# An expert layer's gathered tokens: 72 instead of 64, with GpSimd issuing the small transfers

## The chip, the cores and the metric

The program runs on one core of one Trainium2 chip. The metric is the device time of one execution in microseconds (us), taken as the median over runs. TensorE (PE in the profile) multiplies, VectorE (DVE) and ScalarE (ACT) do the elementwise work, GpSimd (POOL) issues the indirect transfers, and SyncE (SP) issues all the large loads. The engines have one program each, and each runs its own in order.

## The reference, cut to what matters

A two-layer transformer block, a mixer block with cross attention, and a layer of product-key experts run over 256 tokens of width 1024. The change lies in the last of these. Each token picks 16 experts for each of 8 heads, 128 experts in all out of 16384, each with a gate. An expert is a row of `peer_u` and a row of `peer_v`:

```python
act = jax.nn.gelu(jnp.einsum('thkd,td->thk', peer_u[eb], xb), approximate=False) * gb
return jnp.einsum('thk,thkd->td', act, peer_v[eb])
```

So token t gets the sum over its 128 experts of gelu(u·x) · gate · v.

## The kernel before

Everything ahead of `phase_peer` is untouched. In `phase_peer` the 256 tokens go two ways.

**The dense way, 192 tokens (TD).** All 16384 experts are computed for them. A loop of 128 columns j loads one 128x1024 tile of u (512 KB, by SP) for 128 experts and multiplies it with the tokens' x, which is the moving operand. 82 of the columns are plain: 8 chunks of one float32 product of 192 columns (L1648), each of which the trace shows as two passes. The other 46 are split into a high and a low part by ACT (L216) and DVE (L217), which gives 8 pairs of a product of 384 columns (L1650) and one of 192 (L1651). The results stand in A, [128 experts, 128 columns, 192 tokens]. The gates reach A through products of one-hot tables, four tokens at a time (L1531 to L1564, with L1557 on PE); this begins at column J0 = 75, since the end of A holds the routing's tables until then. A second loop of 128 columns does the same with v, always split, in 8 pairs of 384 and 192 columns (L1701, L1702), into eight PSUM banks. At its end a column's sums are halved together, transposed back, added to x, normed and written.

**The gathered way, 64 tokens (TS), the last ones.** Their 128 experts each lie in 64 columns of a table `es` over 128 partitions: partitions 64 to 127 hold a token's second 64 experts, partitions 0 to 63 hold the first 64. The gates lie likewise in `gs`, and `x2` holds the tokens' x twice. A row step gathers 128 rows of u by an indirect transfer from GpSimd (L1474, 512 KB); three steps later DVE multiplies them with `x2` and sums (L1459) into one column of `hs`. After 64 steps come gelu and gates, then 64 steps with rows of v, which DVE adds up weighted (L1464) into `sacc`. At the end the halves are joined: a transfer from SP brings the sums on partitions 0 to 63 to the others (L1486), and DVE adds both to x (L1488, L1490). The rows have four buffers.

**What sets the order.** Every engine's order is fixed when the program is built. `Pace` spreads the row steps over the columns: 33 over columns 12 to 74, 53 over columns 75 to 127, 48 over the first 112 columns of the v loop. A gather also waits for the last product of the column in which it is written (`beat`). The picks of the gathered tokens (`routing(1)`) are made during the projection that precedes the loops and the first 12 columns; `gather(1)` then fills `es` and `gs` by three small transfers from SP (L1424 to L1426), which wait for DVE in SP's queue, ahead of the loads of u that stand behind them. `x2` is filled by one such transfer (L1505).

Of the kernel before, what the change touches and what calls it, by code (L numbers as in the profile page):

```python
# [19 lines left out]
T = 256  # L20
# [81 lines left out]
def layout(I):  # L102
# [91 lines left out]
class K:  # L194
# [12 lines left out]

    def granule(self, ap, w=1024, raw=None):
# [4 lines left out]
        hi = self.ring.tile([128, 1024], F32R, name="hi", bufs=3)  # L213
        lo = self.ring.tile([128, 1024], F32R, name="lo", bufs=3)
# [1092 lines left out]
def phase_peer(k, pool, wpool, out):  # L1307
# [5 lines left out]
    TS = 64  # L1313
    TD = T - TS
    S0 = 128 - TS
# [24 lines left out]

    es = wpool.tile([128, 64], I32, name="es", bufs=1)
    gs = wpool.tile([128, 64], F32, name="gs", bufs=1)
    hs = wpool.tile([128, 64], F32, name="hs", bufs=1)
    x2 = wpool.tile([128, D], F32, name="x2", bufs=1)

# [60 lines left out]
    def gather(tt):  # L1406
# [11 lines left out]
        if tt == 1:  # L1418

            own = slice(S0, 128)  # L1420
            e = slot(8, 64).bitcast(I32)
            V.scalar_tensor_tensor(e[own], ri[own, 0:64], 128.0, rj[own, 0:64], op0=OP.mult, op1=OP.add)
            V.scalar_tensor_tensor(es[own], ri[own, 64:128], 128.0, rj[own, 64:128], op0=OP.mult, op1=OP.add)
            nc.sync.dma_start(es[0:S0], e[own])  # L1424
            nc.sync.dma_start(gs[0:S0], bv[own, 0:64])
            nc.sync.dma_start(gs[own], bv[own, 64:128])  # L1426
        ps = k.tp()
# [17 lines left out]
    def behind(i, how):  # L1445
        k.tc.add_manual_dep(i.ins, beat[0].ins.name, mybir.DependencyInfo(how, mybir.DependencyReason.DATA), reason="pace")


    def gathered():
        AHEAD = 3  # L1450
        todo = []
        sacc = None

        def take():
            nonlocal sacc
# [11 lines left out]
            if (kind, c) == ("u", 63):  # L1467
# [17 lines left out]
        low = wpool.tile([128, D], F32, name="row", bufs=4)  # L1485
        nc.sync.dma_start(low[S0:128], sacc[0:S0])  # L1486
        x = k.x[S0:128, 1, :]
        V.tensor_tensor(x, x, sacc[S0:128], OP.add)  # L1488
        yield
        V.tensor_tensor(x, x, low[S0:128], OP.add)  # L1490
        yield

    J0 = 75
    early, late = routing(1), routing(0)
    for c in range(16):
# [3 lines left out]
        if c == 12:  # L1499
# [3 lines left out]
            V.tensor_scalar(xn[1], k.x[:, 1, :], inv[:, 1:2], None, op0=OP.mult)  # L1503
            V.tensor_tensor(x2[S0:128], xn[1][S0:128], gpeer[S0:128], OP.mult)
            nc.sync.dma_start(x2[0:S0], x2[S0:128])  # L1505

# [100 lines left out]
    for c in range(8):  # L1607
        ps = k.tp()
        nc.tensor.transpose(ps[:, 0:128], xn[0][:, c * 128:c * 128 + 128], k.ident)
        nc.tensor.transpose(ps[:, 128:TD], xn[1][0:S0, c * 128:c * 128 + 128], k.ident[0:S0, 0:S0])  # L1610
        col = k.gains[:, GCOL["peer"] + c:GCOL["peer"] + c + 1]
# [105 lines left out]
    last = [column(j) for j in range(128 - LAST, 128)]  # L1717
    oT = A[:, 6:14, :]
    part = A[:, 40:48, :]
# [4 lines left out]
    def turn(c):  # L1724
# [88 lines left out]
```

## Time and profile before

| | us |
|---|---|
| three runs, median | 1751.54 |
| lowest and highest | 1749.48, 1752.36 |
| the profiled execution, its own time | 1753.15 |
| its span, first to last instruction | 1751.4 |
| PE busy | 1711.7 (98%) |
| DVE busy | 1311.6 (75%) |
| ACT busy | 997.6 (57%) |
| POOL busy | 249.5 (14%) |

The time of the profiled execution is 1.75 us longer than its span, and 1.6 us over the median. PE's busy time is a poor guide, because products are pipelined and their ends are modelled. What counts is the step from one product's start to the next, and the places where PE sat idle. The two loops take the last 697 us of the span.

### The profile page before, as it was taken

What the parts mean: (1) busy time and instruction counts of PE and PEld (TensorE: products, weight loads), DVE (VectorE), ACT (ScalarE), POOL (GpSimd) and SP (SyncE); (2) the same over time, 40 slices, a digit from 0 to 9 for tenths busy, and PEclk for the clock granted to TensorE, in tenths of its full rate; (3) what the DMA queues carried; (4) which work ended last, traced back from release to release, by engine and by line L of the source; (5) the groups of instructions that cost most, each with busy time, mean ns of one, the idle gap of its engine ahead of it and who ended that gap; (6) DMA issues with size and microseconds to landing.
All of it is one profiled execution on the core that took longest, in us unless ns stands there. A gap on an engine that the chain in (4) does not pass through costs nothing.

```text
span 1751.4 us, 29395 instructions
## 1 busy us (share of the span) xinstructions
PE 1711.7 (98%) x10902; PEld 1572.5 (90%) x10902; DVE 1311.6 (75%) x2562; ACT 997.6 (57%) x2025; POOL 249.5 (14%) x184
## 2 busy tenths in 40 slices
PE   8999999999999999999999999999999999999997
PEld 6888888888888888988878899999999999999996
DVE  6867886678678857754366689888689998888875
ACT  6646554555555547766545543233589885555554
POOL 2000000000000000132000000222334344233300
PEclk9999999999999999999999999999999999999999
DMA  7436556653566666532356456888979889999962
GB/s 244 126 111 186 182 186 189 177 178 104 150 193 193 187 193 195 169 111 73 97 174 212 128 169 192 313 303 303 321 269 323 292 305 365 348 331 333 326 229 70
DMA packets 105360, 374.40 MB, mean 214 GB/s; under 512 B 12384, under 2 KB 14080, under 8 KB 104832
## 3 DMA queue, kind: packets, MB, share of 16 engines
q1 hardware_dynamic: 86080, 303.31, 53.2%
q0 software_dynamic: 19136, 69.21, 11.1%
q8 instruction: 86, 1.41, 0.3%
q14 instruction: 58, 0.48, 0.1%
HBM read 368.20 MB, written 3.15 MB: 212 GB/s over the span
## 4 chain that ended last, share of the span: by engine, by line
PE 77%; DVE 8%; issue 6%; ACT 4%; DMA 4%; POOL 0%; SPq 0%; ACTq 0%; POOLq 0%; DVEq 0%
PE acc L222 10%; PE acc L224 10%; PE acc L223 10%; PE acc L270 9%; PE acc L1648 8%; PE acc L271 5%; PE tp L1701 4%; PE acc L1701 4%; PE acc L1650 3%; DVE lo L217 2%; DMA raw<-in_u 2%; PE tp L1702 2%; PE acc L1702 2%; PE tp L1557 1%; PE tp L1165 1%
## 5 line engine op out<-in xcount | busy, mean ns | idle before, releaser
L217 DVE TENSOR_TENSOR lo<-raw,hi 128x1024 fp32r<-128x1024 f32 (+2 forms) x438 | 535.0, 1222 | 261.7 <-ACT hi L216 258.0
L216 ACT CAST hi<-raw 128x1024 fp32r<-128x1024 f32 (+2 forms) x438 | 455.6, 1040 | 461.0 <-PE acc L224 152.6
L270 PE MATMUL acc<-xa,hi 128*128 128x512 f32 x704 | 246.9, 396 | 0.0
L271 PE MATMUL acc<-xa,lo 128*128 128x256 f32 x704 | 196.4, 279 | 0.0
L222 PE MATMUL acc<-xa,hi 128*128 128x256 f32 x568 | 165.9, 292 | 0.8 <-ACT hi L216 0.8
L224 PE MATMUL acc<-xa,lo 128*128 128x256 f32 x568 | 162.3, 286 | 1.2 <-DVE lo L217 1.2
L223 PE MATMUL acc<-xa,hi 128*128 128x256 f32 x568 | 162.4, 286 | 0.0
L1648 PE MATMUL acc<-xf,raw 128*128 128x192 f32 x864 | 160.8, 330 | 0.7 <-ACT ub L1662 0.7
L270 PEld LDWEIGHTS acc<-xa,hi 128*128 128x128 f32 x704 | 132.2, 188 | 31.6
L1701 PE MATMUL tp<-xa,hi 128*128 128x384 f32 x504 | 153.9, 361 | 1.0 <-ACT hi L216 1.0
L1701 PE MATMUL acc<-xa,hi 128*128 128x384 f32 x504 | 154.0, 362 | 0.0
L1648 PEld LDWEIGHTS acc<-xf,raw 128*128 128x128 f32 x864 | 140.1, 193 | 1.0 <-ACT ub L1662 0.9
L1474 POOL DMA_INDIRECT row<-in_v,es x64 | 110.1, 1720 | 183.7 <-DVE xa L282 91.9
L271 PEld LDWEIGHTS acc<-xa,lo 128*128 128x128 f32 x704 | 132.6, 188 | 0.0
L1702 PE MATMUL tp<-xa,lo 128*128 128x192 f32 x504 | 126.8, 253 | 3.2 <-DVE lo L217 3.0
L1702 PE MATMUL acc<-xa,lo 128*128 128x192 f32 x504 | 127.0, 252 | 0.0
L1474 POOL DMA_INDIRECT row<-in_urow,es x64 | 83.9, 1311 | 275.2 <-PE tp L1379 86.9
L1650 PE MATMUL acc<-xa,hi 128*128 128x384 f32 x368 | 121.9, 383 | 0.0
L222 PEld LDWEIGHTS acc<-xa,hi 128*128 128x128 f32 x568 | 109.4, 193 | 2.8 <-ACT hi L216 1.2
L224 PEld LDWEIGHTS acc<-xa,lo 128*128 128x128 f32 x568 | 109.1, 192 | 2.1 <-DVE lo L217 1.7
L223 PEld LDWEIGHTS acc<-xa,hi 128*128 128x128 f32 x568 | 109.5, 193 | 0.6 <-issue 0.2
L1702 PEld LDWEIGHTS tp<-xa,lo 128*128 128x128 f32 x504 | 96.3, 192 | 4.6 <-DVE lo L217 4.4
(483 smaller groups left out, 3949.1 us busy)
## 6 DMA issues: line engine op xcount, KB each, us to landing
raw<-in_u SPq DMA_DIRECT2D x100, 512.0 KB
raw<-in_v SPq DMA_DIRECT2D x84, 512.0 KB
raw<-in_gate SPq DMA_DIRECT2D x44, 512.0 KB
raw<-in_up SPq DMA_DIRECT2D x44, 512.0 KB
raw<-in_down SPq DMA_DIRECT2D x44, 512.0 KB
A<-in_v SPq DMA_DIRECT2D x44, 512.0 KB
raw<-in_gates SPq DMA_DIRECT2D x16, 512.0 KB
raw<-in_pq SPq DMA_DIRECT2D x16, 512.0 KB
```

Of the source, the lines that this page charges most:

```text
L216: nc.scalar.copy(hi[:, :w], raw[:, :w])
L217: nc.vector.tensor_tensor(lo[:, :w], raw[:, :w], hi.bitcast(F32)[:, :w], OP.subtract)
L222: mm(ps, ah, bl, start=start, stop=False)
L223: mm(ps, ah, bh, start=False, stop=False)
L224: mm(ps, al, bh, start=False, stop=stop)
L270: mm(ps, wh[:, s], act.both[:, k].rearrange("p a t -> p (a t)"), start=k == 0, stop=False)
L271: mm(ps[:, T:2 * T], wl[:, s], ah[:, k, :], start=False, stop=k == kn - 1)
L1474: i = nc.gpsimd.indirect_dma_start(out=r, out_offset=None, in_=table, in_offset=bass.IndirectOffsetOnAxis(ap=es[:, c:c + 1], axis=0))
L1648: beat[0] = mm(ps[:, :TD], wh[:, s], xf[:, c], start=c == 0, stop=c == 7)
L1650: mm(ps[:, :2 * TD], wh[:, s], xs[c], start=c == 0, stop=False)
L1701: mm(acc[c][:, 0:2 * TD], vh[:, s], m, start=j == 0, stop=False)
L1702: beat[0] = mm(acc[c][:, 0:TD], vl[:, s], m[:, 0:TD], start=False, stop=j == 127)
```

## The change

Eight more tokens are gathered (TX = 8), so that the dense way has 184 tokens instead of 192. The eight are spread wider than the 64: each lies on 16 partitions with 8 experts on each, in eight further columns of `es`, `gs` and `hs` (COLS = 72). Their x stands 16 times in a second tile `xx`; their weighted rows are summed in a second sum of that name. At the end a product with a constant 0/1 matrix `sel` (L1765 in the new file) adds up the 16 partitions of each token for each of the eight PSUM banks, and ACT copies the 8 columns beside the 184. There are 72 gathers of u and 72 of v. The paces are 36, 61 and 58 instead of 33, 53 and 48, and J0 is 72.

The small transfers of `x2`, `es` and `gs` are issued by GpSimd, and 24 new ones with them: 8 for `xx`, 8 for the eight tokens' experts, 8 for their gates. The join of the 64 tokens' halves starts when their last column is summed, and its second addition is written four row steps later and tied to the column's last product. DVE does one more product for `xx` and one more for the eight tokens' expert numbers.

```diff
-    TD = T - TS
+    TX = 8
+    CX = 128 // TX
+    COLS = TS + TX
+    TD = T - COLS
...
-            nc.sync.dma_start(es[0:S0], e[own])
-            nc.sync.dma_start(gs[0:S0], bv[own, 0:64])
-            nc.sync.dma_start(gs[own], bv[own, 64:128])
+            nc.gpsimd.dma_start(es[0:S0, 0:64], e[own])
+            nc.gpsimd.dma_start(gs[0:S0, 0:64], bv[own, 0:64])
+            nc.gpsimd.dma_start(gs[own, 0:64], bv[own, 64:128])
+
+            e = slot(9, 128).bitcast(I32)
+            low = slice(S0 - 32, S0)
+            V.scalar_tensor_tensor(e[low], ri[low], 128.0, rj[low], op0=OP.mult, op1=OP.add)
+            for dst, src in ((es, e), (gs, bv)):
+                for t in range(TX):
+                    nc.gpsimd.dma_start(dst[t * CX:t * CX + CX, 64:COLS],
+                                        src[S0 - TX + t:S0 - TX + t + 1, :].rearrange("p (r c) -> p r c", c=TX))
...
-                i = V.scalar_tensor_tensor(r, r, 1.0, x2, op0=OP.mult, op1=OP.mult, accum_out=hs[:, col])
-            elif c == 0:
-                sacc = wpool.tile([128, D], F32, name="x2", bufs=1)
-                i = V.tensor_scalar(sacc, r, hs[:, col], None, op0=OP.mult)
+                i = V.scalar_tensor_tensor(r, r, 1.0, x2[c >= TS], op0=OP.mult, op1=OP.mult, accum_out=hs[:, col])
+            elif c in (0, TS):
+                sacc[c >= TS] = wpool.tile([128, D], F32, name="xx" if c else "x2", bufs=1)
+                i = V.tensor_scalar(sacc[c >= TS], r, hs[:, col], None, op0=OP.mult)
             else:
-                i = V.scalar_tensor_tensor(sacc, r, hs[:, col], sacc, op0=OP.mult, op1=OP.add)
+                a = sacc[c >= TS]
+                i = V.scalar_tensor_tensor(a, r, hs[:, col], a, op0=OP.mult, op1=OP.add)
...
-            for c in range(64):
+            for c in range(COLS):
...
-        nc.sync.dma_start(low[S0:128], sacc[0:S0])
+        nc.sync.dma_start(low[S0:128], sacc[0][0:S0])
+        spread.append(sacc[1])
         x = k.x[S0:128, 1, :]
-        V.tensor_tensor(x, x, sacc[S0:128], OP.add)
-        yield
-        V.tensor_tensor(x, x, low[S0:128], OP.add)
-        yield
-
-    J0 = 75
+        V.tensor_tensor(x, x, sacc[0][S0:128], OP.add)
+        for _ in range(4):
+            yield
+
+        behind(V.tensor_tensor(x, x, low[S0:128], OP.add), mybir.DependencyClass.NoSync)
+        yield
+
+    J0 = (128 * TD - 16 * T - 2048 - 4096) // TD
...
-            nc.sync.dma_start(x2[0:S0], x2[S0:128])
+            nc.gpsimd.dma_start(x2[0][0:S0], x2[0][S0:128])
+            low = slice(S0 - 32, S0)
+            V.tensor_tensor(gpeer[low], xn[1][low], gpeer[low], OP.mult)
+            for t in range(TX):
+                nc.gpsimd.dma_start(x2[1][t * CX:t * CX + CX],
+                                    gpeer[S0 - TX + t:S0 - TX + t + 1, None, :].to_broadcast([1, CX, D]))
...
-    rows_early = Pace(rows, 33, J0 - FIRST)
-    rows_late = Pace(rows, 53, 128 - J0)
-    rows_v = Pace(rows, 48, 112)
+    rows_early = Pace(rows, 36, J0 - FIRST)
+    rows_late = Pace(rows, 61, 128 - J0)
+    rows_v = Pace(rows, 58, 112)
...
+        mm(acc[c][:, 2 * TD:2 * TD + TX], spread[0][:, c * 128:c * 128 + 128], sel, start=True, stop=True)
         nc.scalar.copy(part[:, c], acc[c][:, TD:2 * TD])
-        V.tensor_tensor(oT[:, c], acc[c][:, 0:TD], part[:, c], OP.add)
+        V.tensor_tensor(oT[:, c, 0:TD], acc[c][:, 0:TD], part[:, c], OP.add)
+        nc.scalar.copy(oT[:, c, TD:192], acc[c][:, 2 * TD:2 * TD + TX])
```

GpSimd's program from the last norm ahead of the loops to the gathers, before (`rs_r` is an inverse norm, `row` a gathered tile):

```order
L294 TENSOR_TENSOR rs_r_9070<-rs_m_9068,mhalf 128x4
L294 TENSOR_TENSOR rs_r_9162<-rs_m_9160,mhalf 128x4
L294 TENSOR_TENSOR rs_r_9730<-rs_m_9728,mhalf 128x2
L294 TENSOR_TENSOR rs_r_10354<-rs_m_10352,mhalf 128x2
L1474 DMA row<-in_urow,es 128x1024 x64
L1474 DMA row<-in_v,es 128x1024 x64
```

The same place of GpSimd's program now (`x_10381` is `x2`; the tiles named A are the routing's tables):

```order
L294 TENSOR_TENSOR rs_r_10354<-rs_m_10352,mhalf 128x2
L1522 DMA x_10381<-x_10381 64x1024
L1526 DMA xx<-row 16x1x1024 x8
L1429 DMA es<-A 64x64
L1438 DMA es<-A 16x1x8 x4
L1430 DMA gs<-A 64x64
L1431 DMA gs<-A 64x64
L1438 DMA es<-A 16x1x8 x4
L1438 DMA gs<-A 16x1x8 x8
L1488 DMA row<-in_urow,es 128x1024 x72
L1488 DMA row<-in_v,es 128x1024 x72
```

28 transfers stand ahead of the first gather, 19 of them behind the end of the eight tokens' routing.

SP's program around column 12 of the u loop, before and now (the loads at L212 and L213 are those of split columns, at L1519 and L1541 those of plain ones):

```order
L1519 DMA raw_11377<-in_u 128x1024
L1424 DMA es<-A 64x64
L1519 DMA lo<-in_u 128x1024
L1425 DMA gs<-A 64x64
L1426 DMA gs<-A 64x64
L1519 DMA raw<-in_u 128x1024
L212 DMA raw<-in_u 128x1024 x2
```

```order
L1541 DMA raw_11416<-in_u 128x1024
L1541 DMA raw<-in_u 128x1024
L1541 DMA lo<-in_u 128x1024
L213 DMA raw<-in_u 128x1024 x2
L1541 DMA raw_11532<-in_u 128x1024
```

The three small transfers have left SP's queue, and loads of u follow each other.

DVE's program in the v loop where the two halves' sums are joined, before (`x_14273` is `sacc`, `row` the half that the transfer brings):

```order
L1464 SCALAR_TENSOR_TENSOR x_14273<-row,hs,x_14273 128x1024
L217 TENSOR_TENSOR lo<-A,hi 128x1024
L1488 TENSOR_TENSOR x<-x,x_14273 64x1024
L282 TENSOR_TENSOR xa<-A,xa 128x192
L1490 TENSOR_TENSOR x<-x,row 64x1024
L217 TENSOR_TENSOR lo<-raw,hi 128x1024
L282 TENSOR_TENSOR xa<-A,xa 128x192
```

And now, with the 55 rows between the two additions left out but for the ends:

```order
L1478 SCALAR_TENSOR_TENSOR x_14244<-row,hs,x_14244 128x1024
L217 TENSOR_TENSOR lo<-raw,hi 128x1024
L282 TENSOR_TENSOR xa<-A,xa 128x184
L1503 TENSOR_TENSOR x<-x,x_14244 64x1024
L217 TENSOR_TENSOR lo<-A,hi 128x1024
...
L282 TENSOR_TENSOR xa<-A,xa 128x184
L1507 TENSOR_TENSOR x<-x,row 64x1024
L217 TENSOR_TENSOR lo<-A,hi 128x1024
```

The second addition stood two rows behind the first, and now stands 57 rows behind it.

## Rows read from the trace of the kernel before

**Rows 1.** Stages A:B: length, then PE, PEld, DVE, ACT, POOL busy (x); clock, DMA, GB/s.
```profile
1054.74:1094.42 39.68, 38.80 (x243) 37.35 (x242) 37.07 (x153) 13.91 (x31) 0.00 (x0) 1.00 0.60 186
1094.42:1253.64 159.22, 156.97 (x1022) 156.53 (x1021) 127.39 (x368) 53.37 (x120) 40.61 (x33) 1.00 0.88 311
1253.64:1437.27 183.63, 178.52 (x1234) 176.70 (x1233) 165.18 (x324) 160.63 (x485) 68.58 (x52) 0.98 0.86 297
1437.27:1680.90 243.63, 243.21 (x1698) 242.39 (x1698) 209.59 (x265) 138.03 (x216) 84.73 (x44) 1.00 0.94 334
1680.90:1751.40 70.50, 55.51 (x370) 53.24 (x368) 40.45 (x58) 30.52 (x51) 0.72 (x1) 0.91 0.36 120
```

**Rows 2.** The page, part 2: GB/s in 40 slices of 43.8 us.
```profile
GB/s 244 126 111 186 182 186 189 177 178 104 150 193 193 187 193 195 169 111 73 97 174 212 128 169 192 313 303 303 321 269 323 292 305 365 348 331 333 326 229 70
```

**Rows 3.** The chain that ended last, early u columns: start, us, what.
```profile
1061.00 14.63 PE acc L1648 x90
```

**Rows 4.** Timeline, PE, pairs in the v loop and in an earlier layer: start, us, instruction.
```profile
249.87 0.40 PE L270 MATMUL acc<-xa,hi 128*128 128x512 f32 x1
...
255.88 0.40 PE L270 MATMUL acc<-xa,hi 128*128 128x512 f32 x1
...
1619.46 0.36 PE L1701 MATMUL tp<-xa,hi 128*128 128x384 f32 x1
...
1621.74 0.36 PE L1701 MATMUL tp<-xa,hi 128*128 128x384 f32 x1
```

**Rows 5.** Timeline, PE, late u columns: one token's gate product and what follows.
```profile
1350.36 0.39 PE L1557 MATMUL tp<-oj,oi 128*128 128x128 f32 x2
1350.58 0.82 PE L1648 MATMUL acc<-xf,hi 128*128 128x192 f32 x4
```

**Rows 6.** Timeline of SP, DVE and PE where the halves' sums are joined.
```profile
1675.72 0.47 SPq L1486 DMA_DIRECT2D row<-x  x1
...
1681.22 1.22 DVE L1490 TENSOR_TENSOR x<-x,row 64x1024 f32<-64x1024 f32 x1 [2.75 <-DMA row<-x]
...
1683.75 0.36 PE L1702 MATMUL tp<-xa,lo 128*128 128x192 f32 x1 [2.49 <-DVE lo L217]
...
1685.43 0.58 PE L1701 MATMUL acc<-xa,hi 128*128 128x384 f32 x1
...
1685.96 0.57 PE L1701 MATMUL acc<-xa,hi 128*128 128x384 f32 x1
```

**Rows 7.** Waits: SP's queue for DVE, and PE for a load: total, times, longest.
```profile
SPq L1424 <- DVE es L1423: 3.1, 1, 3.1
...
PE tp L1429 <- DMA raw<-in_u: 0.5, 1, 0.5
```

**Rows 8.** GpSimd's issues by tile: a direct transfer, then the gathers: min/median/max ns.
```profile
L806 POOL DMA_DIRECT2D mk_d<-mkt x8: 542/563/784, 147.8 to 452.3; - x8
...
L1474 POOL DMA_INDIRECT row<-in_urow,es x64: 939/1189/2015, 1094.7 to 1364.9; - x64
...
L1474 POOL DMA_INDIRECT row<-in_v,es x64: 939/1912/4507, 1367.9 to 1658.6; - x64
```

**Rows 9.** Timeline: the first gather, and DVE's first use of gathered rows.
```profile
1094.75 1.09 POOL L1474 DMA_INDIRECT row<-in_urow,es  x1 [86.95 <-PE tp L1379]
...
1110.81 1.22 DVE L1459 SCALAR_TENSOR_TENSOR row<-row,x 128x1024 f32<-128x1024 f32 x1
```

**Rows 10.** DVE's groups in columns 75 to 127 of u: busy, mean ns, idle before.
```profile
L1459 DVE SCALAR_TENSOR_TENSOR row<-row,x 128x1024 f32<-128x1024 f32 x34 | 41.4, 1219 | 0.2 <-DMA row<-in_urow,es 0.2
L1531 DVE TENSOR_TENSOR oi<-iota,IT 128x512 f32<-128x512 f32 x46 | 31.4, 683 | 0.0
```

**Rows 11.** Timeline, ACT and PE, where a late load stops column 84.
```profile
1287.89 1.04 ACT L216 CAST hi<-raw 128x1024 fp32r<-128x1024 f32 x1 [3.51 <-DMA raw<-in_u]
...
1289.60 0.80 PE L1557 MATMUL tp<-oj,oi 128*128 128x128 f32 x2 [3.11 <-ACT oj L1542]
```

**Rows 12.** PE's waits in the v loop and the tail: total, times, longest.
```profile
PE tp L1728 <- DVE A L1743: 2.2, 4, 1.0
```

More of the change, by code (lines that the diff above doesn't have):

```diff
@@ L172, in layout @@
     out["v"] = I["peer_v_2"][0].reshape(128, 128, 1024)
+    out["sel"] = np.repeat(np.eye(8, dtype=np.float32), 16, axis=0)
     out["urow"] = np.ascontiguousarray(I["peer_u_2"][0])
@@ L205, in dump, with granule @@
             self.dumps[name] = tuple(ap.shape)
-    def granule(self, ap, w=1024, raw=None):
+    def granule(self, ap, w=1024, raw=None, parts=None):
         nc = self.nc
@@ L212, in granule @@
         nc.sync.dma_start(raw[:, :w], ap)
-        hi = self.ring.tile([128, 1024], F32R, name="hi", bufs=3)
-        lo = self.ring.tile([128, 1024], F32R, name="lo", bufs=3)
+        hi, lo = parts or [self.ring.tile([128, 1024], F32R, name=n, bufs=3) for n in ("hi", "lo")]
         with self.tc.high_priority(self.lead):
@@ L1339, in phase_peer @@
     IT, JT, GT, NJT, NGT = (wpool.tile([128, TD], F32, name=n, bufs=1) for n in ("IT", "JT", "GT", "NJT", "NGT"))
[L1341 to L1344, printed above, removed]
+    es = wpool.tile([128, COLS], I32, name="es", bufs=1)
+    gs = wpool.tile([128, COLS], F32, name="gs", bufs=1)
+    hs = wpool.tile([128, COLS], F32, name="hs", bufs=1)
+    x2 = [wpool.tile([128, D], F32, name=n, bufs=1) for n in ("x2", "xx")]
+    sel = wpool.tile([128, TX], F32, name="sel", bufs=1)
+    nc.sync.dma_start(sel, I["sel"])
     def broadcast_row(dst, n):
@@ L1422, in gather @@
             V.scalar_tensor_tensor(e[own], ri[own, 0:64], 128.0, rj[own, 0:64], op0=OP.mult, op1=OP.add)
-            V.scalar_tensor_tensor(es[own], ri[own, 64:128], 128.0, rj[own, 64:128], op0=OP.mult, op1=OP.add)
-            nc.sync.dma_start(es[0:S0], e[own])
-            nc.sync.dma_start(gs[0:S0], bv[own, 0:64])
-            nc.sync.dma_start(gs[own], bv[own, 64:128])
+            V.scalar_tensor_tensor(es[own, 0:64], ri[own, 64:128], 128.0, rj[own, 64:128], op0=OP.mult, op1=OP.add)
+            nc.gpsimd.dma_start(es[0:S0, 0:64], e[own])
[8 more added lines that the diff above has]
+                                        src[S0 - TX + t:S0 - TX + t + 1, :].rearrange("p (r c) -> p r c", c=TX))
         ps = k.tp()
@@ L1446, in behind @@
         k.tc.add_manual_dep(i.ins, beat[0].ins.name, mybir.DependencyInfo(how, mybir.DependencyReason.DATA), reason="pace")
+    spread = []
     def gathered():
@@ L1451, in gathered @@
         todo = []
-        sacc = None
+        sacc = [None, None]
         def take():
-            nonlocal sacc
             kind, c, r = todo.pop(0)
@@ L1503, in phase_peer @@
             V.tensor_scalar(xn[1], k.x[:, 1, :], inv[:, 1:2], None, op0=OP.mult)
-            V.tensor_tensor(x2[S0:128], xn[1][S0:128], gpeer[S0:128], OP.mult)
-            nc.sync.dma_start(x2[0:S0], x2[S0:128])
+            V.tensor_tensor(x2[0][S0:128], xn[1][S0:128], gpeer[S0:128], OP.mult)
+            nc.gpsimd.dma_start(x2[0][0:S0], x2[0][S0:128])
[4 more added lines that the diff above has]
+                                    gpeer[S0 - TX + t:S0 - TX + t + 1, None, :].to_broadcast([1, CX, D]))
     turns = [0]
@@ L1609, in phase_peer @@
         nc.tensor.transpose(ps[:, 0:128], xn[0][:, c * 128:c * 128 + 128], k.ident)
-        nc.tensor.transpose(ps[:, 128:TD], xn[1][0:S0, c * 128:c * 128 + 128], k.ident[0:S0, 0:S0])
+        nc.tensor.transpose(ps[:, 128:128 + S0], xn[1][0:S0, c * 128:c * 128 + 128], k.ident[0:S0, 0:S0])
         col = k.gains[:, GCOL["peer"] + c:GCOL["peer"] + c + 1]
@@ L1717, in phase_peer @@
     last = [column(j) for j in range(128 - LAST, 128)]
-    oT = A[:, 6:14, :]
+    oT = flat[:, 6 * TD:6 * TD + 8 * 192].rearrange("p (c t) -> p c t", c=8)
     part = A[:, 40:48, :]
@@ L1728, in turn @@
         nc.tensor.transpose(tps[0][:, s], oT[:, c, 0:128], k.ident)
-        nc.tensor.transpose(tps[1][0:S0, s], oT[:, c, 128:TD], k.ident)
+        nc.tensor.transpose(tps[1][0:S0, s], oT[:, c, 128:192], k.ident)
         if c % 4 == 3:
```

2 lines of the change are left out of this document (1 added, 1 removed).

## The prediction

> **What bounds the kernel now.** I read the stages first. In the two loops PE is issuing almost without a break (157.0 of 159.2 us in the early u columns, 243.2 of 243.6 in most of the v loop), so the loops last as long as PE's products step [rows 1]. But two others stand close behind. DVE is busy 165.2 of the 183.6 us of the late u columns, and the DMA engines are busy 0.94 of most of the v loop at 334 GB/s [rows 1], while the best 43.8 us slice of the whole run moved 365 GB/s [rows 2]. The change takes columns from PE and gives row steps to DVE and DMA. So the sum has three parts: what PE saves, which stalls go, and what the tighter neighbours give back.
>
> **Narrower plain products.** 90 passes of a plain column take 14.63 us, 162.6 ns each [rows 3]. A pass holds 192 columns and will hold 184. If all of the step scales, that is 6.8 ns less, if only the slope found below for pairs counts (two cycles a column), 5.7. There are 82 plain columns of 16 passes, 1312: 7.5 to 8.9 us. I take 8.7, near the upper end, since a plain step is nearly all columns.
>
> **Narrower pairs.** Seventeen pairs of 512 and 256 columns take 6.01 us, 353.5 ns each, eight pairs of 384 and 192 take 2.28 us, 285 ns each [rows 4]. That is 68.5 ns for 192 columns, 0.357 ns a column, and 24 columns fewer (16 and 8) make 8.6 ns. If the short product is held up by the next weights, so that only the long one shrinks, it is 16 columns at the 0.423 ns of a plain pass, 6.8 ns; if all 24 count at that price, 10.2. Pairs: 46 split columns and 128 of v, 8 each, 1392. 9.4 to 14.1 us, and I take the slope between the two kinds of pairs, 11.9.
> What the trace shows is that a pair gets shorter by more than two thirds of the bare column time. The Trainium skill (TensorE: Matmul & The Clock Gate, Back-to-back issue gap) gives a sustained spacing of some 81 ns a product at 128 columns and 131 at 512, set by weight loads and products together; that slope, 0.13 ns a column, speaks against this change: an estimate by it is 3.1 ns a pair, 4.3 us. The trace does not bear that slope out, its pairs differ by 0.357; it is the last rival below.
>
> **Gates.** One token's gate costs 1350.58 − 1350.36 = 0.22 us of PE [rows 5]. Eight tokens fewer: 1.8 us.
>
> **The join.** Before, SP issues the halves' transfer at 1675.72, and DVE, which meets its second addition two rows after the first, waits for it 2.75 us, until 1681.22. The split of the next v tile stands behind it in DVE's order, so PE stands 2.49 us. After that its steps are long: a pair takes 0.53 us instead of 0.285 [rows 6], a granted clock of 1.2 GHz, for some six pairs, 1.5 us. In the new order 57 rows stand between the additions, some 24 columns of v, more than 50 us for a transfer that took 5.5. The wait goes: 4.0 us. Behind it nothing is late: loads and splits there run at their pace. The first addition becomes no dearer, since it moves into columns where DVE has room (209.6 of 243.6 us).
>
> **SP's queue freed.** The transfer of the experts held SP for 3.1 us, and PE waited 0.5 us for the load behind it [rows 7]. Gain 0 (loads ahead covered it) to 3.1 (all of it reached PE); I take 0.7, near PE's own wait.
>
> **GpSimd's new issues.** Nine (x2, xx) fall into time in which it idles. Nineteen stand between the end of the routing, at about 1090, and the first gather. A direct transfer takes GpSimd 0.56 us, a gather 1.2 to 1.9, at most 4.5 [rows 8]. 19 x 0.56 = 10.7 us: the first gather goes from 1094.75 to some 1101, and with a landing like the join's 5.5 us it is there at 1106.5. DVE asks at 1110.81 [rows 9], so there are 4 us to spare: the point from which DVE waits is 0.56 + 4/19 = 0.78 us an issue. I take 0.5 us of loss; the other end is the second rival. DVE's own two additions (about 1.2 and 0.2 us, as the like products) fall into a stage where it is busy 37.1 of 39.7 us: 1.0 us, from 0 to 1.5.
> The trace has no direct issue beside the loops' DVE work: the gathers in u and v, 1.2 and 1.9 us, are its only hint that GpSimd gets slower there. The Trainium skill (SBUF — State Buffer, A bandwidth-pool intuition that's wrong) says that a transfer issued from GpSimd waits for its descriptors while DVE holds their shared port, 0.62 us becoming 3.1, which speaks against moving small transfers there; at 3.1 us the estimate for 19 would be 59 us. No run here shows that for a direct transfer.
>
> **More row steps.** In the late u columns there are 61 instead of 53, each of 1.2 us of DVE and more [rows 10]: +10 us. Two of 48 groups of gates go (0.68 us for the table, as much again for the product with A: −2.7), a split column comes (+1.6). DVE goes from 165.2 to 174 us. PE's length there: 53 columns become 56 (J0 = 72), three columns of about 2.5 us (+7.5), narrower products and gates −7: about 184, as before. DVE is then at 95%, and moved bytes go from (53 + 53) to (56 + 61) tiles, 297 to 328 GB/s. How a late load hurts is in the trace: ACT waited 3.51 us for a tile of u, PE stood 3.11 us behind the gate table that ACT makes [rows 11], and the clock was at 1.2 GHz for a while after, some 6.5 us in all. One such stall more or less is the swing: −6 (the present one goes) to +12 (two more). I take +4. In v the bytes per column rise by (1 + 58/112)/(1 + 48/112), 6.2%, and the time falls by 3%: 334 becomes 366 GB/s, just the best slice. 0 to +12 (below), I take +2: before, PE hardly waited there at 334.
>
> **The tail.** 8 small products of two passes (0.11 us each, 1.8 us) and 8 copies of 8 columns come into the last columns, where PE already waits 2.2 us in transposes for the halves' sums [rows 12]. Between 0 (they fit into that wait) and 3.4 us (all in a row); I take 1.5.
>
> **Sum.** 8.7 + 11.9 + 1.8 + 4.0 + 0.7 = 27.1 gained; 0.5 + 1.0 + 4 + 2 + 1.5 = 9.0 given back: −18.1. From the profiled execution's 1753.15 that is 1735.0; its like in the runs is the median, 1.6 lower, so 1733.4: I say 1734.
>
> **Rivals.**
> 1. DMA becomes the bound in v, and late loads in u (the change gives DMA 4% more in 3% less time). At 348 GB/s, the second best slice, the first 107 v columns take 243.6 x 334 x 1.062 / 348 = 248 us, where PE alone wants 236: 12 us go, instead of the 2 booked: 1744. For it: engines busy 0.94. Against: 365 was reached, and buffers kept PE from waiting.
> 2. GpSimd's issues are slow. At 1.9 us, a v gather's, the 19 take 36 us, the first rows land at about 1132, and DVE, in its order, stands 21 us at a row step with the split of the next tile behind it; PE does the plain columns that are loaded and then stands as well, and the clock falls. −18 − 0.5 + 21 + 3 for the clock: 1757, slower. It decides from about 1.5 us an issue, where the wait eats the whole gain. The port lock that the Trainium skill tells of (SBUF — State Buffer, as above) would be its cause.
> 3. Nothing tightens: the stall of column 84 goes and v stays at PE's pace: −18 − 4 − 6 − 2 = −30, 1721.5, and 1723 with a little of it kept.
> 4. The pairs don't shrink, because weight loads set their step: −18 + 11.9 = 1746. By the estimate from the Trainium skill's slope (TensorE: Matmul & The Clock Gate, as above) 4.3 us of it would stay.
> That the transfers don't leave SP, or that the scheduler puts the additions together again, is ruled out by the order of the rows.
>
> **How the numbers follow.** Forecast 0.52 (1728 to 1741), rival 1 0.18, rival 2 0.10, rival 3 0.13, rival 4 0.07. For 8 in 10 the range leaves out rival 2 and the lower half of rival 3, and takes in the others with their spread: 1723 to 1750. About 0.2%, 3.5 us, is what a measurement tells from no change. Faster by more: the forecast, rival 3, and nearly all of 1 and 4, 0.84; within: 0.06, the upper ends of 1 and 4; slower: 0.10.
>
> **What would show it.** Right: plain passes at 155 to 157 ns, pairs at 275 to 278; no wait of DVE for the halves' transfer; the first gather near 1101 and no DVE wait at the first row step; v columns at 2.21 us. Wrong: pairs at 284 (rival 4); ACT waiting for loads of v with PE behind it, over 3 us in all (rival 1); GpSimd's direct issues over 0.8 us and DVE idle ahead of the first row step (rival 2); more than one stall like column 84's.

## The result, and the profile after

The changed kernel is slower: 1760.8 us, median of five runs (1754.0 to 1764.5), against 1750.8 before; the ratio is 1.0066, 95% interval 1.0047 to 1.0085. The forecast was 1734, 1723 to 1750. The trace shown here is of the quickest of the five, 1754.0, with a span of 1752.3; a second one (first experiment) has 1760.2.

Windows of the changed kernel, columns as in [rows 1]: u columns 0 to 12, 13 to 71, 72 to 127, v columns 0 to 123, and the last four with the tail.

```profile
1052.66:1104.36 51.70, 41.63 (x242) 39.89 (x242) 38.56 (x155) 13.68 (x30) 6.40 (x14) 0.87 0.65 164
1104.36:1259.72 155.36, 147.20 (x974) 145.85 (x973) 127.65 (x372) 49.80 (x116) 49.79 (x49) 0.99 0.84 311
1259.72:1445.07 185.35, 178.89 (x1266) 175.09 (x1265) 172.32 (x336) 159.13 (x479) 81.27 (x60) 1.00 0.92 327
1445.07:1725.90 280.83, 279.05 (x1986) 277.80 (x1986) 244.47 (x307) 159.36 (x247) 71.82 (x49) 1.00 0.91 326
1725.90:1752.30 26.40, 14.55 (x98) 12.41 (x96) 11.16 (x23) 9.37 (x28) 0.72 (x1) 0.82 0.11 41
```

The table (us) has the kernel before cut at the same columns, in its first trace and in that of experiment 14, and the forecast by stage, which is the prediction's own terms laid out: 6.6 ns less a plain pass, 8.6 a pair, the gates, the row steps' 4 and the join in their stages.

| stage | before, 1st trace | before, 2nd trace | forecast | after, 1st trace | after, 2nd trace |
|---|---|---|---|---|---|
| u 0 to 12 | 39.7 | 39.7 | 39.1 | 51.7 | 50.1 |
| u 13 to 71 | 151.7 | 152.8 | 146.4 | 155.4 | 155.6 |
| u 72 to 127 | 191.1 | 185.8 | 188.2 | 185.4 | 188.0 |
| v 0 to 123 | 289.0 | 293.7 | 278.4 | 280.8 | 286.6 |
| rest | 25.2 | 25.2 | 26.4 | 26.4 | 26.3 |
| sum | 696.7 | 697.1 | 678.5 | 699.6 | 706.7 |

Two stages, the first 13 columns and the 59 after them, miss by 22 us in one trace and by 20 in the other. The late columns and the tail are as forecast; v misses by 2 to 8. A stage of the same kernel differs by up to 6 us from one execution to the next, so one trace alone settles only what is larger than that.

**The first columns.** PE's longest wait in them (total, times, longest):

```profile
PE acc L1670 <- DMA raw<-in_u: 7.9, 1, 7.9
```

Its place in PE's timeline:

```profile
1065.81 2.35 PE L1670 MATMUL acc<-xf,lo 128*128 128x184 f32 x14
1076.01 6.21 PE L1670 MATMUL acc<-xf,raw 128*128 128x184 f32 x24 [7.85 <-DMA raw<-in_u]
```

And SP's timeline ahead of it, a row that covers three issues and the time between them; below it all issues of that line in the run (min/median/max ns):

```profile
1055.34 12.16 SPq L1541 DMA_DIRECT2D raw<-in_u  x3
...
L1541 SPq DMA_DIRECT2D raw<-in_u x54: 327/328/5079, 883.7 to 1422.9; - x54
```

PE stands 7.85 us for a load of u. The longest issue of SP takes 5.08 us, where the median is 0.33. The granted clock is 0.87 over the stage (1.00 before). The DMA queues from 1055 to 1072 (MB, share of 16 engines) say why:

```profile
q0 software_dynamic: 334, 0.78, 64.1%
q1 hardware_dynamic: 516, 1.88, 31.2%
...
raw<-in_u SPq DMA_DIRECT2D x4, 512.0 KB, 14.3
xx<-row POOLq DMA_DIRECT2D x2, 64.0 KB, 14.3
```

GpSimd's queue, with `x2` (a third of its bytes, read from 64 partitions) and the eight transfers of `xx`, moves 0.78 MB and holds the 16 DMA engines for 0.641 x 16 x 17 = 174 us of engine time (engine-us), 4.5 GB/s an engine; the loads beside it get 22 (1.88 MB in 85). Loads of u take 14.3 us to land.

**The products** got shorter. 32 plain passes in the chain that ended last:

```profile
1240.37 5.01 PE acc L1670 x32
```

Two pairs of v in PE's timeline, eight apart:

```profile
1600.53 0.35 PE L1723 MATMUL tp<-xa,hi 128*128 128x368 f32 x1
...
1602.77 0.36 PE L1723 MATMUL tp<-xa,hi 128*128 128x368 f32 x1
```

156.6 ns a pass against 162.6 [rows 3], forecast 155 to 157. A pair takes 280 ns against 285 [rows 4], forecast 275 to 278: half of what was booked.

**GpSimd's issues**, from its timeline:

```profile
1101.24 0.54 POOL L1429 DMA_DIRECT2D es<-A  x1 [42.18 <-DVE A L1435]
...
1106.83 3.81 POOL L1438 DMA_DIRECT2D gs<-A  x8
1110.95 1.30 POOL L1488 DMA_INDIRECT row<-in_urow,es  x1 [0.31 <-issue]
```

DVE's first use of a gathered row, which follows without a wait:

```profile
1120.85 1.22 DVE L1472 SCALAR_TENSOR_TENSOR row<-row,x 128x1024 f32<-128x1024 f32 x1
```

Nineteen issues take 9.4 us, 0.5 each, beside DVE's work. All of it lies 10 us late only because the routing does.

### The profile page after: what moved, and what is told of

It is laid out like the page before. It is cut to its first block, busy times and chain, and to the rows that moved or that the text cites. A ratio compares the mean times of both kernels' runs of the same rounds, so it can differ in the third digit from the quotient of the medians.

```text
span 1752.3 us, 29491 instructions
## 1 busy us (share of the span) xinstructions
PE 1700.1 (97%) x10902; PEld 1557.6 (89%) x10902; DVE 1325.7 (76%) x2585; ACT 992.1 (57%) x2022; POOL 266.0 (15%) x228
## 3 DMA queue, kind: packets, MB, share of 16 engines
q0 software_dynamic: 22384, 78.45, 12.8%
## 4 chain that ended last, share of the span: by engine, by line
PE 68%; DVE 12%; issue 8%; DMA 7%; ACT 3%; POOL 0%; ACTq 0%; POOLq 0%; SPq 0%; DVEq 0%
PE acc L222 10%; PE acc L224 10%; PE acc L223 10%; PE acc L270 9%; PE acc L271 5%; DMA raw<-in_u 4%; PE acc L1670 4%; PE acc L1723 3%; PE tp L1723 3%; DVE lo L217 3%; DMA raw<-in_v 2%; ACT hi L216 1%; PE tp L1724 1%; PE acc L1724 1%; PE tp L1165 1%
## 5 line engine op out<-in xcount | busy, mean ns | idle before, releaser
L216 ACT CAST hi<-raw 128x1024 fp32r<-128x1024 f32 (+2 forms) x438 | 455.6, 1040 | 465.4 <-PE acc L224 152.8
L1670 PE MATMUL acc<-xf,raw 128*128 128x184 f32 x864 | 154.7, 324 | 10.8 <-DMA raw<-in_u 10.8
L1723 PE MATMUL tp<-xa,hi 128*128 128x368 f32 x504 | 150.7, 357 | 1.0 <-ACT hi L216 1.0
L1723 PE MATMUL acc<-xa,hi 128*128 128x368 f32 x504 | 150.4, 356 | 0.0
L1670 PEld LDWEIGHTS acc<-xf,raw 128*128 128x128 f32 x864 | 136.0, 193 | 11.8 <-issue 11.6
L1488 POOL DMA_INDIRECT row<-in_v,es x72 | 103.7, 1440 | 174.0 <-DVE xa L282 54.8
L1724 PE MATMUL tp<-xa,lo 128*128 128x184 f32 x504 | 125.7, 249 | 2.1 <-DVE lo L217 1.9
L1724 PE MATMUL acc<-xa,lo 128*128 128x184 f32 x504 | 125.1, 248 | 0.0
L1672 PE MATMUL acc<-xa,hi 128*128 128x368 f32 x368 | 119.6, 380 | 0.0
L1488 POOL DMA_INDIRECT row<-in_urow,es x72 | 93.1, 1293 | 167.5 <-PE acc L1670 43.2
```

The costliest lines, as they stand in the source:

```text
L1488: i = nc.gpsimd.indirect_dma_start(out=r, out_offset=None, in_=table, in_offset=bass.IndirectOffsetOnAxis(ap=es[:, c:c + 1], axis=0))
L1670: beat[0] = mm(ps[:, :TD], wh[:, s], xf[:, c], start=c == 0, stop=c == 7)
L1672: mm(ps[:, :2 * TD], wh[:, s], xs[c], start=c == 0, stop=False)
L1723: mm(acc[c][:, 0:2 * TD], vh[:, s], m, start=j == 0, stop=False)
L1724: beat[0] = mm(acc[c][:, 0:TD], vl[:, s], m[:, 0:TD], start=False, stop=j == 127)
```

## Experiments

Medians against the kernel before on the same chip (1749 to 1750); where a run had one execution, that is said. Stage times are from each run's trace.

**1. The changed kernel again.** 

> The changed kernel itself once more, for a second trace. The first trace was the quickest of five executions (1754.0, the others 1759.9 to 1764.5). In it u columns 0 to 12 took 51.7 us where the kernel before takes 39.7, with PE standing 8 us at one load, and columns 13 to 71 lost some 14 us in stalls where the kernel before loses 6. Theory A (eight transfers of xx, each of which reads one SBUF partition 16 times, hold the DMA engines): columns 0 to 12 at 50 to 54 us again, packets of these transfers above 2 us again. If the first columns come out near 40 us, the stall was an accident of that execution and theory A falls.

1761.6, ratio 1.0067 (1.0044 to 1.0089); stages in the table. The first columns take 50.1 us again: theory A stands.

**2. Sixteen source partitions instead of one.**

```diff
-    nc.gpsimd.dma_start(x2[1][t * CX:t * CX + CX],
-                        gpeer[S0 - TX + t:S0 - TX + t + 1, None, :].to_broadcast([1, CX, D]))
+    u = (t + TX // 2) % TX
+    nc.gpsimd.dma_start(x2[1][t * CX:t * CX + CX], gpeer[u * CX:u * CX + CX])
```

> The eight transfers of xx stay with GpSimd, of the same size and in the same place, but each takes its 16 rows from 16 partitions instead of one (the second x of the eight added tokens is then not theirs). Theory A (one source partition): packets at 0.2 to 0.5 us as x2's, columns 0 to 12 at 38 to 40 us, the whole run some 12 us below the changed kernel's. Theory B (GpSimd's queue takes the DMA engines from the loads, whatever it carries): columns 0 to 12 at 50 us and more, no change. Theory C (only the bytes count, 0.8 MB at some 400 GB/s): 2 us less at most.

1748.8, 12.8 us below the changed kernel; columns 0 to 12 take 39.7. But the edit does not keep the transfers in their place. Six of the eight now read partitions that the last product ahead of them does not write, and GpSimd issues them long before the loops:

```profile
888.83 3.01 POOL L1527 DMA_DIRECT2D xx<-row  x6 [18.05 <-DMA row<-in_rows]
```

Only two and `x2` are left in the stage. The same queues from 1055 to 1072:

```profile
q1 hardware_dynamic: 810, 2.97, 59.4%
q0 software_dynamic: 144, 0.39, 8.9%
...
raw<-in_u SPq DMA_DIRECT2D x5, 512.0 KB, 4.0
```

The transfers left there move 0.39 MB in 24 engine-us, 16 GB/s an engine, and loads land in 4.0 us instead of 14.3. The six early ones, from 888 to 895:

```profile
q0 software_dynamic: 179, 0.37, 19.3%
```

That is 0.37 MB in 22 engine-us (0.193 x 16 x 7), 17 GB/s. So in either place sixteen source partitions go at 16 to 17 GB/s an engine, from the same queue and with the same size; at that rate all nine transfers would hold some 49 engine-us instead of 174 (an estimate). How much of the 12.8 us is the source and how much that six transfers have left the stage, this run can't tell, and it doesn't by itself refute theories B and C.

**3. `x2` and `xx` issued by SP.** `nc.sync` for `nc.gpsimd` in those nine. 

> The transfers of x2 and xx are issued by SP again, the small ones of experts and gates stay with GpSimd. Theory A (one source partition): packets above 2 us again, columns 0 to 12 at 50 us or more, since the loads of u now stand behind them in the same queue; no faster than the changed kernel. Theory B (GpSimd's queue): columns 0 to 12 near 39 us, some 12 us below the changed kernel.

1754.6; columns 0 to 12 take 46.0, so the transfers stay dear from SP too, but half as dear: theory A's 50 was too high. In SP's order the first loads go ahead of them; that this halves the price is argued. From 1055 to 1068 the queue carries little but `xx`:

```profile
DMA packets 206, 0.42 MB, mean 32 GB/s; under 512 B 103, under 2 KB 103, under 8 KB 206
...
q1 hardware_dynamic: 206, 0.42, 92.2%
```

The 16 engines are busy 0.92 of the time and move 32 GB/s, 2.2 an engine. That is the one source partition without GpSimd's queue: theory B (the queue) falls, and so does theory C (the bytes), since 0.42 MB hold the engines for 13 us.

**4. The rows spread by PE.**

```diff
+    pick = wpool.tile([128, 128], F32, name="oj", bufs=4)[low]
+    nc.scalar.copy(pick.rearrange("p (t c) -> p t c", c=CX), k.ident[low, S0 - TX:S0, None].to_broadcast([32, TX, CX]))
+    for nb in range(2):
+        ...
+        mm(ps, pick, gpeer[low, n], start=True, stop=True)
+        nc.scalar.copy(x2[1][:, n], ps)
```

> No transfers for xx: PE spreads the eight rows with two products of 32 rows by 128 (a copy of the identity's columns) and 512 columns, and ACT copies them from PSUM, both in u column 4. Theory A and B alike: columns 0 to 12 at 38 to 40 us, 12 us below the changed kernel or more, 1746 to 1750. If the other stalls of the u columns (8 us more than before) come from the late start too, 1738 to 1744; if they come from the row steps, they stay.

1753.9, in all 8 us below the changed kernel instead of the 12 expected: columns 0 to 12 take 41.8, and columns 13 to 71 come out at 159.1. The other stalls do not come from the late start; they stay.

**5. Other paces for the row steps**, with the products of the fourth in column 11.

```diff
-    rows_early = Pace(rows, 36, J0 - FIRST)
-    rows_late = Pace(rows, 61, 128 - J0)
-    rows_v = Pace(rows, 58, 112)
+    rows_early = Pace(rows, 33, J0 - FIRST)
+    rows_late = Pace(rows, 53, 128 - J0)
+    rows_v = Pace(rows, 69, 121)
```

> As the run in which PE spreads the eight rows (now in u column 11, ahead of transposes for which PE stands 1.8 us anyway), and with other paces of the row steps: 33 in the early u columns and 53 in the late ones, as before the change, and 69 over 121 columns of v instead of 58 over 112. Theory D (the added row steps make u's loads late): columns 13 to 71, at 154 to 159 us in the traces of the changed kernels, come to 147 to 150; v pays for it, 0.785 MB a column are 351 GB/s, some 3 to 6 us; in all 1745 to 1750. Theory E (the narrower columns alone are too quick for the loads): columns 13 to 71 stay at 154 and more, v loses, 1754 to 1760.

1736.8, ratio 0.9934 (0.9916 to 0.9951): faster than before, and better than theory D's own figure. Columns 13 to 71 and 72 to 127 as windows, first in the fourth run (36 and 61 row steps), then in this one (33 and 53):

```profile
1095.48:1254.61 159.13, 148.69 (x974) 146.74 (x973) 127.69 (x372) 50.00 (x116) 49.15 (x49) 0.98 0.83 304
1254.61:1441.54 186.93, 178.65 (x1267) 175.04 (x1265) 172.25 (x336) 158.98 (x479) 79.23 (x59) 1.00 0.91 325
...
1094.25:1242.15 147.90, 145.01 (x974) 144.12 (x973) 124.08 (x365) 49.62 (x115) 42.42 (x43) 1.00 0.85 312
1242.15:1422.74 180.59, 177.61 (x1267) 175.00 (x1265) 164.52 (x332) 159.44 (x479) 68.20 (x53) 1.00 0.90 317
```

11 us go in the early columns and 6 in the late ones, and v, with 286 against 289, loses nothing.

**6. The eight tokens' gathers left out.** `for c in range(TS)`, paces 33, 53 and 50. 

> Left out: the row gathers of the eight added tokens (64 gathers in u and in v, not 72) and so their sums; the narrower products stay, paces 33, 53 and 50 over 112. Theory D (the added row steps): columns 13 to 71 at 146 to 148, the late u columns from 72 on at 182 or less, v columns 0 to 123 at 280 to 282: 1735 to 1739. Theory E (narrower columns are too quick for the loads): columns 13 to 71 at 153 or more, 1745 and more.

1734.1, ratio 0.9912 (0.9891 to 0.9932); columns 13 to 71 at 148.2, v at 283.1, a little over theory D's 282. By the medians the eight tokens' rows, well placed, cost 2.7 us in all; the two runs' intervals overlap.

**7. More row steps than 36.** 39 in the early columns, 63 in v. 

> As the run with paces 33, 53 and 69 (1736.8), but 39 row steps in the 60 early u columns and 63 in v. The step from 36 to 33 took 11 us out of columns 13 to 71 (159.1 to 147.9). Theory D1 (the number of row steps: more bytes and more of DVE a column): 39 are worse than 36, columns 13 to 71 at 160 or more, 1745 and above. Theory D2 (36 in 60 is three in five, the same period as the split columns, so that every period has its row steps at the same two or three columns and a late load comes back each time): 39, which drift against it, are better than 36, columns 13 to 71 at 152 or less, 1737 to 1742.

1747.9, columns 13 to 71 at 160.7: the number counts, not its beat (D1). How a stall forms is seen in this run. SP's waits from 1205 to 1225 (total, times, longest):

```profile
SPq L213 <- DVE lo L217: 17.5, 2, 10.9
```

SP's timeline, two issues that follow each other:

```profile
1211.55 0.33 SPq L1538 DMA_DIRECT2D hi<-in_u  x1
1222.81 0.33 SPq L213 DMA_DIRECT2D raw<-in_u  x1
```

DVE's timeline before the second of them:

```profile
1212.74 0.35 DVE L1691 TENSOR_TENSOR ub<-acc,ub 128x184 f32<-128x184 f32 x1 [4.95 <-ACT ub L1690]
...
1220.14 1.20 DVE L1472 SCALAR_TENSOR_TENSOR row<-row,x 128x1024 f32<-128x1024 f32 x1
...
1221.53 1.21 DVE L217 TENSOR_TENSOR lo<-raw,hi 128x1024 fp32r<-128x1024 f32 x1
```

PE's timeline, later:

```profile
1230.03 1.45 PE L1676 MATMUL acc<-xf,hi 128*128 128x184 f32 x5 [3.38 <-DVE ub L1691]
```

DVE has first stood 4.95 us for ACT, which had itself waited for a load. Then it reaches the split of a tile only behind routing steps and two row steps. Until it is through, the tile's buffer isn't free, SP's next load waits 10.9 us, and all loads behind it with it. PE's 3.4 us columns later end with DVE as well: L1691 empties the accumulator that PE needs, and DVE has worked up to it without a gap. Of PE's waits from 1094 to 1275, 8.3 us are for this step of DVE and 2.1 for loads of u.

**8. The paces alone in the changed kernel.** 

> The changed kernel with nothing but the other paces, 33, 53 and 69 over 121; the eight transfers of one partition each stay. If the causes add up, the transfers' 12 us stay and the paces' 12 to 17 go: columns 0 to 12 at 50 to 52, columns 13 to 71 at 147 to 150, 1745 to 1750. If the late start of the rows was what made the u columns stall, columns 13 to 71 stay at 154 and more, and 1755 to 1760.

1746.6, 15.0 us below the changed kernel's 1761.6, with columns 0 to 12 at 51.5, 13 to 71 at 151.9 and 72 to 127 at 180.0. These two runs lie on different chips; set against the kernel before on its own chip each time, the paces bring 13.9 us, and paces and transfers together, in the fifth, 24.2. With the 12.8 of the second the two causes add up, nearly. The early columns give only 3.5 of it here, the late ones 5 to 8.

**9. DVE or DMA?** The run with 39 row steps, with DVE's products cut, then with gathers left out; one execution each.

```diff
+    w = slice(0, 32 if c < 36 else D)
-    i = V.scalar_tensor_tensor(r, r, 1.0, x2[c >= TS], op0=OP.mult, op1=OP.mult, accum_out=hs[:, col])
+    i = V.scalar_tensor_tensor(r[:, w], r[:, w], 1.0, x2[c >= TS][:, w], op0=OP.mult, op1=OP.mult, accum_out=hs[:, col])
```

> As the run with 39 row steps in the early u columns, but DVE's part of the first 36 u rows is cut from 1024 columns to 32 (left out: most of their products with x), while their gathers stay. Theory H (DVE's time is what the early u columns lack: a row step of 1.2 us holds back the split of a tile, and with it the buffer for which SP's next load waits): columns 13 to 71, 160.7 us with whole products, come to 146 to 149. Theory I (the DMA engines' time: gathers of 0.5 MB hold up the loads): they stay at 157 and more.

> The counterpart: 39 row steps, DVE's products whole, but of the first 36 u rows only four are gathered (left out: the others' gathers; their products use the four again). Theory H (DVE): columns 13 to 71 stay at 156 and more. Theory I (DMA): 146 to 149. If both runs come out near 150, the two add up, and neither alone is the cause.

Columns 13 to 71 as windows, first with 39 whole row steps:

```profile
1095.33:1256.00 160.67, 148.25 (x975) 145.81 (x973) 131.07 (x377) 49.21 (x115) 47.73 (x47) 0.99 0.83 306
```

With DVE's products cut:

```profile
1095.70:1247.22 151.52, 146.96 (x975) 145.73 (x973) 94.78 (x377) 49.92 (x115) 45.50 (x49) 0.99 0.88 328
```

With few gathers:

```profile
1096.53:1246.43 149.90, 146.72 (x974) 145.79 (x973) 130.82 (x377) 50.28 (x115) 11.44 (x14) 0.99 0.64 218
```

36 us less of DVE bring 9 us, a third of the bytes less (306 x 160.7 to 218 x 149.9) brings 11, to the same 150. So neither H nor I: it takes both, since either part taken away brings the columns to where 33 row steps have them. That a load late by DVE's order hurts because the gathers then delay it further is an argument, not shown.

**10. v's row steps, fewer in the first 40 columns.** 

> As the run with paces 33, 53 and 69, but the 69 row steps of v are 16 in the first 40 columns and 53 in the next 81 (they were spread evenly). All of v's stalls in the traces lie in columns 3 to 39; from column 40 on every other load has a buffer of its own in the gates' table. Theory G (the first 40 columns have too few buffers for a late load): v columns 0 to 123, 286.3 before this, come to 280 to 283, 1731 to 1734, though columns 40 to 121 then ask for 0.83 MB each, 370 GB/s. Rival: DMA is the bound there, stalls appear after column 40, 1737 and more.

> As the last, with three row steps fewer in the late u columns (50) and 56 over 82 columns in the second part of v: 0.84 MB a column, 376 GB/s. The late u columns gain 0.5 to 1.5 us by the stalls at gate products, v loses 0 to 3: 1730 to 1735.

1734.1 and 1730.0, ratios 0.9914 (0.9896 to 0.9933) and 0.9910 (0.9890 to 0.9931): v takes 281.7 and 279.5, and nothing stalls after column 40, in the second at 387 to 396 GB/s in the slices there. The rival falls. Theory G fits, but isn't shown: the eighth run, which spreads the same 69 steps evenly, has v at 282.4. What the traces do show is where v's time varies: columns 40 to 123 take 188 us in every trace with 184 tokens but one (the eleventh run), whatever the pace of the row steps, and columns 0 to 39 take 91 to 101. The second has the lowest median of all versions; its windows, with the first four stages:

```profile
1052.74:1094.01 41.27, 39.32 (x247) 36.67 (x246) 38.67 (x156) 14.89 (x33) 4.71 (x10) 1.00 0.62 197
1094.01:1243.45 149.44, 145.12 (x975) 144.12 (x973) 124.05 (x365) 49.38 (x115) 42.32 (x43) 1.00 0.85 309
1243.45:1422.11 178.66, 177.27 (x1267) 175.01 (x1265) 160.82 (x329) 159.42 (x479) 63.34 (x50) 1.00 0.88 312
1422.11:1701.64 279.53, 278.49 (x1987) 277.75 (x1986) 258.16 (x320) 159.49 (x247) 69.77 (x62) 1.00 0.94 352
```

**11. Fewer early steps still, 28.** 

> As the same run, with 28 row steps in the early u columns (33), 52 in the late ones, 17 in the first 40 of v and 58 in the next 82 (0.85 MB a column, 382 GB/s). If the stalls of columns 13 to 71 go on falling with the row steps (18.7 us at 39, 13.9 to 17.7 at 36, 6.8 to 10.9 at 33), 4 to 6 us are left, 1727 to 1730. If what is left at 33 is the routing's own (the kernel before has 5.9 and 6.9), the columns stay at 148 and v pays, 1730 to 1734.

1737.1 (1733.5 to 1743.0). In the one trace the early columns take 146.2, as hoped, but v takes 288.1: a gather's issue, 1.2 us at this run's median, took ten there, in GpSimd's timeline:

```profile
1584.70 10.27 POOL L1488 DMA_INDIRECT row<-in_v,es  x1 [2.89 <-PE acc L1733]
```

and DVE waited for its row:

```profile
DVE x L1478 <- DMA row<-in_v,es: 7.4, 1, 7.4
```

Why it took ten is open, and so is whether it explains the other executions, whose lowest is 1733.5.

**12. The small transfers back to SP**, in the best version. 

> As the best run so far (1730.0: eight rows spread by PE, paces 33, 50, 16 and 56), but the transfer of x2 and the nineteen of experts and gates are issued by SP again, as before the change. The prediction's term: SP freed 0.7 us, from 0 to 3.1, for three transfers; now there are nineteen in a row at some 0.5 us, nearly 10 us in which SP issues no load of u. If the loads ahead cover it: 1730 to 1732. If not, PE stands at the loads behind them, 4 to 8 us more, 1734 to 1738.

1733.8, ratio 0.9908 (0.9871 to 0.9944), 3.8 us above the best version by medians, but on another chip; against the kernel before on its own chip it does as well (0.9910 there). In the trace columns 13 to 71 take 154.7 instead of 149.4. SP's timeline:

```profile
1093.47 4.38 SPq L1438 DMA_DIRECT2D es<-A  x7
1097.90 5.02 SPq L1438 DMA_DIRECT2D gs<-A  x8
```

For 9.4 us SP issues no load of u. In columns 13 to 71 ACT waits 24.7 us for loads instead of 14.3, as the second branch said, yet PE itself only 0.3. 33 row steps had these columns anywhere from 147.9 to 151.9 in the other traces, and the ratio is no worse: that nineteen small transfers need GpSimd as issuer is not shown.

**13. The short product of a pair.** `vl[:, s], m[:, 0:128]` for `m[:, 0:TD]` in the kernel before; one execution. 

> The kernel before with the short products of the v pairs cut from 192 columns to 128 (the correction of 64 tokens is left out in v). Columns set the step: a pair falls by 64 columns at 0.417 ns, from 284.4 to 258 ns. Theory F (a short product has a floor, that of the next weight load, and 192 columns are already at it): a pair stays at 280 to 285 ns, and what the change gains in a pair is the long product's 16 columns alone, 6.7 ns.

Two pairs of v in PE's timeline, eight apart:

```profile
1599.63 0.39 PE L1701 MATMUL tp<-xa,hi 128*128 128x384 f32 x1
...
1601.92 0.39 PE L1701 MATMUL tp<-xa,hi 128*128 128x384 f32 x1
```

286 ns a pair, against 284 or 290 with 192 columns (experiment 14): 64 columns fewer save nothing that stands out from these two paces. So the short product's length no longer sets the step at 192; that the next weights do is argued, not shown.

**14. The join alone**, in the kernel before; then, one execution each, the kernel before and the join alone again.

```diff
-    yield
-    V.tensor_tensor(x, x, low[S0:128], OP.add)
+    for _ in range(4):
+        yield
+    behind(V.tensor_tensor(x, x, low[S0:128], OP.add), mybir.DependencyClass.NoSync)
```

> The kernel before with nothing but the second addition four row steps later (and 50 row steps of v for 48, so that they are all placed). The prediction's term: the stall at v column 106 goes, 4.0 us, a ratio of 0.9977. Rival: something else ends there as late, no change, 1.000.

> The kernel before once more, for a second trace: its v columns run at two paces, 2.275 us (from column 39 on) and 2.32 us (columns 9 to 30); the kernel with the join alone ran at 2.32 from column 39 on, which took back the 4 us of its missing stall. Theory J (the pace is an accident of an execution): either pace may come; the stall at v column 106 is there with 4 us. Theory K (the order of the instructions sets the pace): 2.275 from column 39 on again.

> The second addition four row steps later alone, again, for a second trace. Theory J (accident): 2.275 or 2.32. Theory K (order): 2.32 from column 39 on again, so that the join's 4 us are always taken back.

Ratio 0.9997 (0.9983 to 1.0011): the forecast 0.9977 lies outside, the 4 us do not show in the medians. In the traces the stall is gone, but v's columns have two paces, whatever the kernel: from column 39 on 2.275 us before and 2.32 before again, 2.32 with the join and 2.275 with the join again. At the same pace v takes 289.0 before and 284.0 with the join (5 us less), at the other 293.7 and 293.0, where the join's run stalled 3 us more ahead of column 40. Theory J: the pace is an accident, worth 4 us. What sets it is open, and so is why twelve runs don't show the gain. The stall itself comes back in the second trace of before, column 106:

```profile
1681.95 0.35 PE L1702 MATMUL tp<-xa,lo 128*128 128x192 f32 x1 [2.09 <-DVE lo L217]
```

## Why the prediction was wrong, point by point

**The step that failed first** is "Nine (x2, xx) fall into time in which it idles". It counted GpSimd's time to issue them and not the transfers, which share the DMA engines with the loads of u. Eight of them read one partition 16 times each, hold the engines (2.2 GB/s an engine in the third run) and make the loads behind them late: 12.0 us in the first columns (51.7 − 39.7), 10 of which are gone in the fourth, without these transfers. The Trainium skill (SBUF — State Buffer, Door 1: The DMA port swizzle) says that a transfer's rate goes by how many of SBUF's 16 ports its partitions reach, some 27 GB/s each. The eight rows lie in partitions 56 to 63, two ports of its table; by that an estimate for 0.52 MB is 9.6 us. The trace of the third run agrees: its 32 GB/s lie between the rates of one port and of two. The rule would have warned.

**The second** is "More row steps". It priced the late u columns and v, and put the early columns at nothing without a reason, though 36 steps in 60 columns replace 33 in 63. DVE is busy 0.80 of them [rows 1], but that share is a mean: in the seventh run DVE works 18 us without a gap, and what SP and PE wait for stands in that row. The early columns came out 9 us above the forecast. With 39, 36, 33 and 28 steps the columns 13 to 71 take 160.7, 154 to 159, 148 to 152 (154.7 in the twelfth run) and 146.2, while the u loop of the kernel before has 151.7 to 156.1 in five traces: the number of steps is shown as the cause, the way from a late split to PE's wait only in part.

In the late u columns the value, 185 to 188 for a forecast of 188, was right in part by luck. The forecast started from 191.1, which has the stall of column 84; the second trace of the kernel before has 185.8 without it. And the added steps cost some 5 to 8 us there, more than the +4 booked: with 33 early and 53 late steps these columns take 180 to 181 (runs 5, 6, 8 and 10).

**The third is a size, pairs.** 11.9 us were booked, 8.6 ns each. Against the pace that the forecast had read, v's pairs gave 4.6 ns (2.275 to 2.238 us a column), 4.7 us of the 8.8 booked for v, which is below the lower bound as well. The kernel before has a second pace, 2.32, and against that one they gave 10. The slope between 512/256 and 384/192 columns holds only where the short product's length still counts; at 192 it no longer does (run 13), so that only the long one's 16 columns would shorten the step; no run tells the two apart at 184. The rival "the pairs don't shrink" was half right. The estimate of 3.1 ns a pair from the Trainium skill's slope (TensorE: Matmul & The Clock Gate, Back-to-back issue gap) was nearer to 4.6 than the forecast's 8.6.

**v** took 281 to 287 us in the two traces of the changed kernel, 278 booked. The pairs account for 4 us, more than the first trace missed by. What the second lost beyond that is in the first 40 columns, which take 92.8 and 98.6 us in the two traces, where their pace alone would give 89.5. There ACT waits 22 and 33 us for loads, and PE for the splits behind them. The prediction's "buffers kept PE from waiting" holds only from column 40 on, where the two traces lose nothing: DMA as the bound in v, the first rival, did not come.

**The join** was booked with 4.0 us. The stall is gone in every trace with the change, but alone the edit gains nothing that the medians show (0.9983 to 1.0011). What takes the gain back is open.

**Right.** Plain passes at 156.6 ns. GpSimd's issues at 0.5 us each and no wait of DVE at the first row; the lock between DVE and GpSimd's descriptors that the second rival feared (the Trainium skill, SBUF — State Buffer, A bandwidth-pool intuition that's wrong) does not appear beside this DVE work. The tail (+1.2). The best version's sum of stages, 674.9 us, lies 3.6 below the forecast's 678.5. It has other paces and spreads the eight rows by PE, so a gain of the forecast's size was there to be had, under two costs that were not seen.

## What to carry to other kernels

Cost a small transfer on the DMA engines too, by what it reads: many copies of one partition hold all the engines, whoever issues them, and stall the loads behind. Read an engine's room in the stretch where its order is tightest, not from its mean, and put added work where more of it leaves the pace alone (here v from column 40 on). Before a step is scaled with columns, find the width below which it stops shrinking. And see in a trace that an experiment's edit moved nothing but what it was to move: the second run's six early transfers don't show in its time.

## What the runs showed of the hardware

Transfers of 64 KB within SBUF moved at 2.2 GB/s an engine when each read one partition sixteen times (issued by SP, the engines busy 0.92), and at 16 to 17 when each read sixteen partitions (issued by GpSimd). A pair of products of 384 and 192 columns takes 284 or 290 ns, with 128 in the short one 286. The same v columns ran at 2.275 or 2.32 us from one execution to the next, constant over 67 and more columns; with 184 tokens all traces show 2.24. A gather's issue once took 10.27 us, where its run's median is 1.2.
